# A one-core FFN down projection: one more seven-product step in the last column pair, later pair-end loads, two additions deferred, a GpSimd scratch tile of its own

## The chip, the cores and the metric

The kernel runs on one NeuronCore of one Trainium2 chip. The metric is the device time of one execution in microseconds (us). The engines are named as the profile names them: PE is TensorE (matrix products), PEld its weight loads, DVE is VectorE, ACT is ScalarE, POOL is GpSimd, and SP is SyncE, which here only issues DMAs. DMAs are issued from two queues: SP's (q1 in the profile) and POOL's (q0); only POOL's can add to what lies at the destination.

## The reference, cut to what matters

The kernel computes one decoder layer in float32 over 256 tokens: a normalisation, one input projection, eight retention heads and four mLSTM heads, an output projection, and then the part that the change touches, a gated feed-forward network (FFN) and the final normalisation:

```python
u = rmsnorm(h, norm_ffn)
up = causal_dwconv(u @ w_up, ffn_conv_w, ffn_conv_b)      # 2048 -> 2 x 5632
gate, val = jnp.split(up, [FFN_DIM], axis=-1)
h = h + (jax.nn.silu(gate) * val) @ w_down                # 5632 -> 2048
return rmsnorm(h, norm_final)[:, N_META:]
```

## The kernel before, in words

**Splitting.** Every float32 weight tile is split in two: ACT casts it to a reduced format (`whi`), DVE subtracts that from the original (`wlo`, the rest). The activations are split in the same way ahead of time. A product of weights and activations is then three matmuls: high by high, high by low, low by high. A weight tile so costs one ACT cast (L141, or L768 in the down projection's fast steps) and one DVE subtraction (L143, L770). `whi` and `wlo` have five buffers each.

**The FFN** runs in two halves of its 5632 columns. In each half first the up projection (matmuls L150, L151, L153, tiles of 512 KB loaded by L127), then the down projection, which adds to the residual stream `hn` (256 tokens in two row tiles, tt = 0 and 1; 2048 columns in four blocks of 512).

**The down projection** takes two column blocks at a time: pair `b` = 0, then pair `b` = 2. Each pair goes through eleven steps `q` over the half's rows, 256 at a time. There are two kinds of step:

- A *plain* step (0, 9 and 10) loads a raw tile for each of the two blocks (`load_plain`, into `wraw` tiles of side 0 or 1), splits both (two L143) and runs `product` for both row tiles: 24 matmuls of 512 columns (L821, L822, L824).
- A *fast* step (`seven`, steps 1 to 8) does the two-by-two block product with seven products instead of eight (after Winograd): 21 matmuls (L846, L847, L849). It needs sums of weight blocks. Part of them (`kept`) are made long before by DMAs that add in DRAM (class `Early`, four DMAs for a unit, spread over the loads of the up projection by `AHEAD` and its neighbours, with a one-element add on POOL, L210, as pace). One sum more is made by DVE in the step (L832, `ta`); another (`tb`) is loaded from `kept` by `load_sum` (L930, POOL's queue). The step's raw tile sits in `left[0]` or `left[1]`, in the tile named `hT`, and comes in three DMAs (`load_seven`, L909 by way of `load`, SP's queue). Its splits are three L770 of 1024 columns and one of 512.

Below, (b, q) is a step of a pair: hT(2,1) is the raw tile of pair 2's step 1.

**The end of a pair.** After the last fast step `share` combines the seven products' sums in `x` tiles and adds them to `hn` by four accumulating DMAs on POOL's queue (L865). After the last plain step ACT copies the pair's other accumulators out (L1003), and DVE adds them to `hn` (four L1004, which wait for those DMAs).

**The final pair** (half 1, b = 2) is different: the steps in `BOTH` are done plain, and without an early unit, so that some of its last work can be done row tile by row tile. Its order was 0, 1, 6, 2, 7, 3, 4, 5, 8, 9, 10, with 1 to 5 fast. The last four plain steps load and split one block first (one L143, twelve matmuls) and the other block later. Beside the fast steps POOL multiplies finished blocks of `hn` by the final norm's gain `gfin` (`times_gain`, L715), each released by a one-element add (L855). After the last product DVE adds the last pieces (L888), ACT and DVE make the norm's factor (L711, L720, L721, L727 to L731), and L738, L740 (DVE) and L743 (ACT) scale the rows for the output.

**What sets the order.** The program is written in the order of the code, but a list scheduler places each instruction on its engine by its own model of time; what then stands on an engine's queue is fixed, and each engine works through it in order. A DMA queue is in order too: an SP load that waits for its buffer holds all loads behind it. `tc.issue_after` ties an instruction behind another.

`raw_home` tiles have two buffers on each side; in the up projection the side of a load follows from its number: `loads % 4 // 2`.

Of the kernel before, what the change touches and what calls it, by code (L numbers as in the profile page):

```python
# [34 lines left out]
WARM = 8  # L35


AHEAD, AHEAD_STEP, REST, RESUME = 40, 22, 222, 238

# [47 lines left out]
def trunk(ctx: ExitStack, tc: tile.TileContext, io, out: bass.AP):  # L87
# [26 lines left out]


    last_load = None
    loads = paced = 0

    def raw_home(shape, side):
        return wpool.tile(shape, F32, name=f"wraw{side}", bufs=2)  # L120
# [638 lines left out]
    for half in range(2):  # L759
# [66 lines left out]
        def seven(b, q, cs, ps, first, last, after, norm):  # L826


            f = FAST.index(q)
            raw, ta, tb = homes.pop((b, q))  # L830

            nc.vector.tensor_tensor(out=ta, in0=raw[:, 0:1, :].to_broadcast([P, 2, 512]), in1=raw[:, 1:3, :], op=ALU.subtract)  # L832
            copied = None
            for w, to in (
                (raw[:, 2:4, :], ((S4, cs[0, 1], False, False), (A12, cs[0, 0], False, False))),
                (raw[:, 0:2, :], ((S2, ps[2], first, last), (A11, ps[0], first, last))),
                (ta, ((S3, ps[1], first, last), (S1, ps[3], first, last))),
                (tb, ((A22, cs[1, 0], False, False),)),
            ):
                hi = wpool.tile([P, 2, 512], F32R, name="whi", bufs=5)  # L840
                lo = wpool.tile([P, 2, 512], F32R, name="wlo", bufs=5)
                n = len(to)
                with tc.issue_after(after.ins) if first and after else nullcontext():
                    copied, _ = split(hi[:, :n, :], lo[:, :n, :], w)
                for i, (m, o, begin, _) in enumerate(to):
                    nc.tensor.matmul(o, sh[:, f, m, :], hi[:, i, :], start=begin, stop=False)  # L846
                    nc.tensor.matmul(o, sl[:, f, m, :], hi[:, i, :], start=False, stop=False)  # L847
                for i, (m, o, _, end) in enumerate(to):
                    nc.tensor.matmul(o, sh[:, f, m, :], lo[:, i, :], start=False, stop=end)  # L849
            if norm:  # L850

                with tc.issue_after(copied.ins):
                    for g in norm:
                        squares(*g)
                reached = nc.gpsimd.tensor_tensor(out=junk[:, 0:1], in0=tb[:, 0, 0:1], in1=tb[:, 0, 0:1], op=ALU.add)  # L855
                with tc.issue_after(reached.ins):
                    for tt, _, c0, c1 in norm:
                        times_gain(tt, c0, c1)

        def block(tt, b):  # L860
            return hn[:, tt, b * 512 : (b + 1) * 512]
# [40 lines left out]

        homes, raws = {}, {}
        begun = shared = None

        def load(to, src):
            nonlocal begun
# [18 lines left out]
        def load_sum(b, q):  # L926

            tb = sums_home[1][:, FAST.index(q) % 2, :][:, None, :]
# [8 lines left out]
        gains = []  # L937
        emptied = None
        for b in (0, 2):
            cs = {}  # L940
# [17 lines left out]
            for q in steps:  # L958
                if q in fast:
                    due = []  # L960
                    if final and q != fast[0]:
                        due, gains = gains[:1], gains[1:]
                    seven(b, q, cs, ps, q == fast[0], q == fast[-1], emptied, due)
                    if q == fast[-1]:
                        with tc.high_priority() if final else nullcontext():
                            shared = share(ps, b, final)
                else:
                    for j in range(1 if q in alone else 2):
                        w = split_step(raws.pop((b + j, q)))
                        for tt in range(2):  # L970
                            product(cs[tt, j], tt, q, w, q == plain[0], q == plain[-1 - (lag if final and (tt, j) == (1, 1) else 0)])

                if final:
                    if q == 0:
                        load_plain(b, 6, 0)
                    elif q == 6:
                        load_plain(b, 7, 0, 1)
                    elif q in (3, 4, 5):
                        load_plain(b, q + 5, 0 if q < 5 else 1, 1)
                    if q in (1, 2, 3):  # L980
                        load_seven(b, q + 2)
                        load_sum(b, q + 2)
                else:
                    if q == 6:
                        load_plain(b, 9, 0)
                    if q in range(1, 7):
                        load_seven(b, q + 2)
                        load_sum(b, q + 2)
                    if q == 8:
                        load_plain(b, 10, 1)  # L990
                    if b == 0:
                        if q == 7:
                            load_seven(2, 1)
                        elif q == 9:
                            load_plain(2, 0, 0)
                            load_seven(2, 2)
            for j in range(2):
                for n, tt in enumerate(range(2)):
                    c = (b + j) * 512
                    if not final:  # L1000

                        x = x_tile((4, 3, 1, 0)[2 * j + n])
                        emptied = nc.scalar.copy(x, cs[tt, j])  # L1003
                        nc.vector.tensor_tensor(out=block(tt, b + j), in0=block(tt, b + j), in1=x, op=ALU.add)  # L1004
# [117 lines left out]
```

## Time and profile before

| what | value |
|---|---|
| three runs | 1213.59, 1210.86, 1211.42 us (median 1211.42) |
| the profiled execution | 1212.01 us, its span 1210.2 us |
| granted clock of PE, mean | 0.998 |
| PE busy | 1198.8 us (99%) |
| DVE busy | 951.6 us (79%) |
| ACT busy | 713.4 us (59%) |
| POOL busy | 258.7 us (21%) |
| DMA queue q1 (SP) | 239.06 MB, 58.0% of the 16 engines' span |
| DMA queue q0 (POOL) | 37.11 MB, 17.5% |

The profiled execution is one run of its own; its span is the time from the first to the last recorded instruction, and 1.8 us of its device time lie outside. Times inside it are counted from the span's start. A row of the timeline has the start, the duration, the engine, the line and operation, output<-inputs, and how many of them follow one another; in brackets stands the engine's idle time before it and what released it. In rows of DMA issues the time is that of issuing; "to landing" is the time from the issue until the data was there. In this profile the first half's pair change lies at 763 to 779 us, the second half's at 1131 to 1149, and the last matmul at 1202.

### The profile page before, as it was taken

The page shows a single profiled execution, that of the slowest core. Times are in us where ns is not written, and L with a number is a line of the kernel's source. Part 1 is how long each engine was busy: PE and PEld are TensorE (multiplying, and loading weights), DVE is VectorE, ACT ScalarE, POOL GpSimd, SP SyncE. Part 2 cuts the span into 40 slices and gives each one's busy share as a digit, 9 for nine tenths or more (in the row PEclk, how much of TensorE's full clock was granted, in tenths as well). Part 3 has the DMA queues.
Part 4 walks back from the last instruction along what each step waited for, and adds up shares of the span by engine and source line. Part 5 has one row for each costly group of instructions (what it writes and reads, how often), then busy time and mean ns, then how long its engine had stood idle before and what let it go on. Part 6 is the DMA issues. An engine that isn't in the chain of part 4 may idle for free.

```text
span 1210.2 us, 23069 instructions
## 1 busy us (share of the span) xinstructions
PE 1198.8 (99%) x8947; PEld 1150.3 (95%) x8947; DVE 951.6 (79%) x1390; ACT 713.4 (59%) x973; POOL 258.7 (21%) x349
## 2 busy tenths in 40 slices
PE   9999999999999999999999999999999999999997
PEld 9999999999999999999999998878999999998786
DVE  8877778766775867788889779897877777778896
ACT  8657746656556556555555557665655555556673
POOL 0100022223231322233132100101133223300132
PEclk9999999999999999999999999999999999999999
DMA  7765677878786977788887757777888778847955
GB/s 278 263 224 159 203 235 210 254 217 238 209 244 208 260 223 222 238 256 227 237 229 224 233 181 261 229 249 228 271 228 252 240 222 237 221 161 265 291 195 183
DMA packets 102366, 278.50 MB, mean 230 GB/s; under 512 B 16432, under 2 KB 20656, under 8 KB 102128
## 3 DMA queue, kind: packets, MB, share of 16 engines
q1 hardware_dynamic: 84016, 239.06, 58.0%
q0 software_dynamic: 17664, 37.11, 17.5%
q8 instruction: 70, 1.15, 0.4%
q10 hardware_dynamic: 576, 0.85, 0.2%
q14 instruction: 40, 0.33, 0.1%
HBM read 268.59 MB, written 42.47 MB: 257 GB/s over the span
## 4 chain that ended last, share of the span: by engine, by line
PE 95%; DMA 2%; DVE 1%; ACT 0%; issue 0%; SPq 0%; DVEq 0%; ACTq 0%
PE mmps L150 25%; PE mmps L153 25%; PE mmps L151 25%; PE atps L821 2%; PE mmps L849 2%; PE atps L822 2%; PE atps L824 2%; PE mmps L846 2%; PE mmps L847 2%; PE atps L846 1%; PE atps L847 1%; PE atps L849 1%; DMA wraw<-in_wu 1%; DVE wlo L770 1%; DMA hT<-kept 1%; PE atps L444 1%
## 5 line engine op out<-in xcount | busy, mean ns | idle before, releaser
L141 ACT CAST whi<-wraw 128x1024 fp32r<-128x1024 f32 x346 | 361.8, 1049 | 334.0 <-PE mmps L151 221.6
L143 DVE TENSOR_TENSOR wlo<-wraw,whi 128x1024 fp32r<-128x1024 f32 x346 | 430.2, 1246 | 79.0 <-ACT whi L141 74.8
L150 PE MATMUL mmps<-uh,whi 128*128 128x258 f32 x1408 | 345.3, 283 | 0.6 <-ACT whi L141 0.6
L151 PE MATMUL mmps<-ul,whi 128*128 128x258 f32 x1408 | 345.0, 281 | 0.0
L151 PEld LDWEIGHTS mmps<-ul,whi 128*128 128x128 f32 x1408 | 266.6, 189 | 0.1
L150 PEld LDWEIGHTS mmps<-uh,whi 128*128 128x128 f32 x1408 | 265.3, 188 | 0.9 <-ACT whi L141 0.8
L150 PE MATMUL mmps<-xh,whi 128*128 128x272 f32 (+2 forms) x864 | 219.7, 287 | 0.0
L151 PE MATMUL mmps<-xl,whi 128*128 128x272 f32 (+2 forms) x864 | 218.2, 285 | 0.0
L153 PE MATMUL mmps<-uh,wlo 128*128 128x258 f32 x1408 | 197.9, 283 | 0.0
L153 PEld LDWEIGHTS mmps<-uh,wlo 128*128 128x128 f32 x1408 | 181.7, 189 | 0.0
L151 PEld LDWEIGHTS mmps<-xl,whi 128*128 128x128 f32 x864 | 162.6, 188 | 0.0
L150 PEld LDWEIGHTS mmps<-xh,whi 128*128 128x128 f32 x864 | 162.5, 188 | 0.1
L210 POOL TENSOR_TENSOR pace<-whi 128x1 f32<-128x1 f32 x87 | 52.2, 600 | 429.9 <-ACT whi L141 411.8
L153 PE MATMUL mmps<-xh,wlo 128*128 128x272 f32 (+2 forms) x864 | 126.8, 285 | 0.0
L153 PEld LDWEIGHTS mmps<-xh,wlo 128*128 128x128 f32 x864 | 114.5, 188 | 0.0
L697 DVE TENSOR_TENSOR cu<-mmps,rstd 128x258 f32<-128x258 f32 x88 | 37.6, 427 | 72.9 <-PE mmps L153 72.2
L770 DVE TENSOR_TENSOR wlo<-hT,whi 128x1024 fp32r<-128x1024 f32 x58 | 69.3, 1218 | 3.5 <-ACT whi L768 3.5
L768 ACT CAST whi<-hT 128x1024 fp32r<-128x1024 f32 x58 | 59.3, 1049 | 15.7 <-DMA hT<-kept 5.3
L768 ACT CAST whi<-wraw 128x1024 fp32r<-128x1024 f32 (+1 forms) x58 | 46.6, 835 | 35.5 <-DVE wraw L832 17.7
L151 PE MATMUL mmps<-mixl,whi 128*128 128x258 f32 x256 | 63.1, 283 | 0.0
L150 PE MATMUL mmps<-mixh,whi 128*128 128x258 f32 x256 | 62.5, 283 | 0.0
L770 DVE TENSOR_TENSOR wlo<-wraw,whi 128x1024 fp32r<-128x1024 f32 (+1 forms) x58 | 53.2, 952 | 1.5 <-ACT whi L768 0.5
(272 smaller groups left out, 1768.3 us busy)
## 6 DMA issues: line engine op xcount, KB each, us to landing
wraw<-in_wu SPq DMA_DIRECT2D x176, 512.0 KB, 4.5
wraw<-in_wi SPq DMA_DIRECT2D x108, 512.0 KB, 4.5
wraw<-in_wo SPq DMA_DIRECT2D x32, 512.0 KB, 5.4
wraw<-in_wd SPq DMA_DIRECT2D x30, 512.0 KB, 5.6
kept<-in_wd SPq DMA_DIRECT2D x29, 512.0 KB, 6.8
kept<-in_wd POOLq DMA_DIRECT2D x58, 256.0 KB, 6.7
hT<-in_wd SPq DMA_DIRECT2D x29, 512.0 KB, 4.9
kept<-kept POOLq DMA_DIRECT2D x29, 256.0 KB, 5.4
```

The costliest lines, as they stand in the source:

```text
L141: nc.scalar.copy(hi, raw)
L143: nc.vector.tensor_tensor(out=lo, in0=raw, in1=hi.bitcast(F32), op=ALU.subtract)
L150: nc.tensor.matmul(ps, hi[:, k, :], xh(kk), start=kk == first, stop=False)
L151: nc.tensor.matmul(ps, hi[:, k, :], xl(kk), start=False, stop=False)
L153: nc.tensor.matmul(ps, lo[:, k, :], xh(kk), start=False, stop=kk == last)
L210: with tc.issue_after(nc.gpsimd.tensor_tensor(out=pace, in0=x, in1=x, op=ALU.add).ins):
L697: evacuated = nc.vector.tensor_tensor(out=u, in0=ps[:, :NQ], in1=rstd2, op=ALU.mult)
L768: copied = nc.scalar.copy(hi, x)
L770: return copied, nc.vector.tensor_tensor(out=lo, in0=x, in1=hi.bitcast(F32), op=ALU.subtract)
L846: nc.tensor.matmul(o, sh[:, f, m, :], hi[:, i, :], start=begin, stop=False)
L847: nc.tensor.matmul(o, sl[:, f, m, :], hi[:, i, :], start=False, stop=False)
L849: nc.tensor.matmul(o, sh[:, f, m, :], lo[:, i, :], start=False, stop=end)
```

## The change

- `BOTH` is (7, 8) instead of (6, 7, 8): the final pair does steps 1 to 6 fast, in the order 0, 1, 2, 7, 3, 4, 5, 6, 8, 9, 10. One more `Early` unit (30 instead of 29) is made for it, and `AHEAD` goes from 40 to 36 loads. `kept21`, which keeps pieces that the plain steps of `BOTH` need, is a third smaller.
- `loads`, the counter that picks the raw side, starts at 3 instead of 0.
- hT(2,1) was loaded after step 7 of pair 0; now it is loaded after step 9, on SP's queue, behind the plain tiles of steps 10 and (2,0). hT(2,2), which stood there, goes to POOL's queue behind the four accumulating DMAs.
- In the final pair, from step 3 on, `tb` is loaded on SP's queue instead of POOL's.
- Of the four L1004 adds at the end of a pair 0, the two of block j = 1 are put into a list (`later`) and issued behind the last split of pair 2's first fast step.
- `gfin` (1 MB) is no longer loaded at the start of half 1's down projection but in four pieces beside steps 3 to 6 of its first pair.
- The one-element add ahead of `times_gain` writes `pace`, not `junk`, which ACT writes too.

Lines of the FFN's helpers move by one (L143 is L144, L770 is L771, L832 is L833), later ones by more (L930 is L943, L1004 is L1023, L715 and L728 to L740 are one higher, L888 is L890).

```diff
-AHEAD, AHEAD_STEP, REST, RESUME = 40, 22, 222, 238
+AHEAD, AHEAD_STEP, REST, RESUME = 36, 22, 222, 238
...
-    loads = paced = 0
+    loads, paced = 3, 0
...
-    BOTH = FAST[-3:]
+    BOTH = FAST[-2:]
...
-                reached = nc.gpsimd.tensor_tensor(out=junk[:, 0:1], in0=tb[:, 0, 0:1], in1=tb[:, 0, 0:1], op=ALU.add)
+                reached = nc.gpsimd.tensor_tensor(out=pace, in0=tb[:, 0, 0:1], in1=tb[:, 0, 0:1], op=ALU.add)
...
-            nc.gpsimd.dma_start(gfin, io["gfin"])
...
-            load(raw[:, 2:4, :], io["wd7"][b // 2, half * NQD + q][:, 2:4, :])
-            load(raw[:, 1, :], io["wd7"][b // 2, half * NQD + q][:, 1, :])
-            load(raw[:, 0, :], early[b, half * NQD + q].kept[:, 0, :])
+            w = io["wd7"][b // 2, half * NQD + q]
+            parts = ((raw[:, 2:4, :], w[:, 2:4, :]), (raw[:, 1, :], w[:, 1, :]), (raw[:, 0, :], early[b, half * NQD + q].kept[:, 0, :]))
+            for to, src in parts:
+                if (b, q) == (2, 2):
+
+                    with tc.issue_after(shared.ins):
+                        nc.gpsimd.dma_start(to, src)
+                else:
+                    load(to, src)
...
-            with tc.issue_after(shared.ins) if shared else nullcontext():
-                nc.gpsimd.dma_start(tb[:, 0, :], early[b, half * NQD + q].kept[:, 1, :])
+            kept = early[b, half * NQD + q].kept[:, 1, :]
+            if half == 1 and b == 2 and q > 2:
+
+                load(tb[:, 0, :], kept)
+            else:
+                with tc.issue_after(shared.ins) if shared else nullcontext():
+                    summed = nc.gpsimd.dma_start(tb[:, 0, :], kept)
...
-            steps = [0, 1, 6, 2, 7, 3, 4, 5, 8, 9, 10] if final else range(NQD)
+            steps = [0, 1, 2, 7, 3, 4, 5, 6, 8, 9, 10] if final else range(NQD)
...
-                    seven(b, q, cs, ps, q == fast[0], q == fast[-1], emptied, due)
+                    done = seven(b, q, cs, ps, q == fast[0], q == fast[-1], emptied, due)
+                    if q == fast[0]:
+
+                        with tc.issue_after(done.ins):
+                            while later:
+                                later.pop(0)()
...
+                    if (half, b) == (1, 0) and q in range(3, 7):
+                        cols = slice((q - 3) * 512, (q - 2) * 512)
+                        with tc.issue_after(summed.ins):
+                            nc.gpsimd.dma_start(gfin[:, cols], io["gfin"][:, cols])
                     if b == 0:
-                        if q == 7:
+                        if q == 9:
+                            load_plain(2, 0, 0)
                             load_seven(2, 1)
-                        elif q == 9:
-                            load_plain(2, 0, 0)
                             load_seven(2, 2)
...
-                        nc.vector.tensor_tensor(out=block(tt, b + j), in0=block(tt, b + j), in1=x, op=ALU.add)
+                        later.append(lambda to=block(tt, b + j), x=x: nc.vector.tensor_tensor(out=to, in0=to, in1=x, op=ALU.add))
+                        if j == 0 or b == 2:
+                            later.pop(0)()
```

Three places show how instructions move on DVE. The first is the start of half 0's pair 0, where the up projection ends. The first sum (`wraw<-hT`), the plain step's two splits (L143, the last two) and the first fast split stood before like this:

```order
L143 TENSOR_TENSOR wlo<-wraw_9078,whi 128x1024
L697 TENSOR_TENSOR cu<-mmps,rstd_78 128x258
L143 TENSOR_TENSOR wlo<-wraw_9132,whi 128x1024
L701 SCALAR_TENSOR_TENSOR vt<-cu,par,vt 128x256 x2
L782 TENSOR_TENSOR gt<-gt,vt 128x256
L143 TENSOR_TENSOR wlo<-wraw_9134,whi 128x1024
L770 TENSOR_TENSOR ml<-gt,mh 128x256
L832 TENSOR_TENSOR wraw_9142<-hT 128x1024
```

and now:

```order
L144 TENSOR_TENSOR wlo<-wraw_9083,whi 128x1024
L833 TENSOR_TENSOR wraw_9147<-hT 128x1024
L698 TENSOR_TENSOR cu<-mmps,rstd_78 128x258
L144 TENSOR_TENSOR wlo<-wraw_9137,whi 128x1024
L702 SCALAR_TENSOR_TENSOR vt<-cu,par,vt 128x256 x2
L144 TENSOR_TENSOR wlo<-wraw_9139,whi 128x1024
```

The sum moved ahead of the plain step's two splits.

The second is the change from pair 0 to pair 2 in half 0 (half 1 has the same, but for the second sum, which now stands ahead of the 512-column split). `hn<-hn,x` are the adds at the pair's end. Before:

```order
L143 TENSOR_TENSOR wlo<-wraw_9524,whi 128x1024
L143 TENSOR_TENSOR wlo<-wraw_9558,whi 128x1024
L832 TENSOR_TENSOR wraw_9613<-hT 128x1024
L143 TENSOR_TENSOR wlo<-wraw_9560,whi 128x1024
L1004 TENSOR_TENSOR hn<-hn,x_5926 128x512 x4
L770 TENSOR_TENSOR wlo<-hT,whi 128x1024 x2
L770 TENSOR_TENSOR wlo<-wraw_9613,whi 128x1024
L770 TENSOR_TENSOR wlo<-wraw_9614,whi 128x512
L832 TENSOR_TENSOR wraw_9613<-hT 128x1024
```

Now:

```order
L144 TENSOR_TENSOR wlo<-wraw_9526,whi 128x1024
L144 TENSOR_TENSOR wlo<-wraw_9560,whi 128x1024
L144 TENSOR_TENSOR wlo<-wraw_9562,whi 128x1024
L833 TENSOR_TENSOR wraw_9616<-hT 128x1024
L1023 TENSOR_TENSOR hn<-hn,x_5931 128x512 x2
L771 TENSOR_TENSOR wlo<-hT,whi 128x1024 x2
L771 TENSOR_TENSOR wlo<-wraw_9616,whi 128x1024
L771 TENSOR_TENSOR wlo<-wraw_9617,whi 128x512
L1023 TENSOR_TENSOR hn<-hn,x_5931 128x512 x2
L833 TENSOR_TENSOR wraw_9616<-hT 128x1024
```

Two of the adds moved behind step 1's splits, and step 1's sum behind the last plain split.

The third is the end of the program on DVE. The 256-column `hn<-atps,hn` rows are the last adds of row tile 0 and of row tile 1, each followed by links of its norm factor; L740 and L738 scale. Before:

```order
L740 TENSOR_SCALAR hn<-hn,frt 128x256
L740 TENSOR_SCALAR hn<-hn,frt 128x768
L738 SCALAR_TENSOR_TENSOR hn<-hn,frt,gfin 128x512
L720 TENSOR_REDUCE rest<-ss_5925 128x1
L721 TENSOR_SCALAR rest<-rest 128x1
L888 TENSOR_TENSOR hn<-atps,hn 128x256
L728 TENSOR_SCALAR frt<-ss_5925,rest 128x1
```

Now:

```order
L890 TENSOR_TENSOR hn<-atps,hn 128x256
L741 TENSOR_SCALAR hn<-hn,frt 128x256
L741 TENSOR_SCALAR hn<-hn,frt 128x768
L739 SCALAR_TENSOR_TENSOR hn<-hn,frt,gfin 128x512
L729 TENSOR_SCALAR frt<-ss_5930,rest 128x1
```

Row tile 0's scaling moved behind the last add.

More of the change, by code (lines that the diff above doesn't have):

```diff
@@ L843, in seven @@
                 with tc.issue_after(after.ins) if first and after else nullcontext():
-                    copied, _ = split(hi[:, :n, :], lo[:, :n, :], w)
+                    copied, parted = split(hi[:, :n, :], lo[:, :n, :], w)
                 for i, (m, o, begin, _) in enumerate(to):
@@ L858, in seven @@
                         times_gain(tt, c0, c1)
+            return parted
         def block(tt, b):
@@ L903, in trunk @@
         homes, raws = {}, {}
-        begun = shared = None
+        begun = shared = summed = None
         def load(to, src):
@@ L920, in load_seven @@
             turn = 1 - turn
[L921 to L923 removed]
+            w = io["wd7"][b // 2, half * NQD + q]
[6 more added lines that the diff above has]
+                    load(to, src)
             homes[b, q] = raw
         def load_sum(b, q):
+            nonlocal summed
             tb = sums_home[1][:, FAST.index(q) % 2, :][:, None, :]
[L929 to L930 removed]
+            kept = early[b, half * NQD + q].kept[:, 1, :]
[4 more added lines that the diff above has]
+                    summed = nc.gpsimd.dma_start(tb[:, 0, :], kept)
             homes[b, q] = homes[b, q], sums_home[0], tb
@@ L936, in trunk @@
         lag = 4
-        gains = []
+        gains, later = [], []
         emptied = None
@@ L974, in trunk @@
                     if q == 0:
-                        load_plain(b, 6, 0)
-                    elif q == 6:
                         load_plain(b, 7, 0, 1)
-                    elif q in (3, 4, 5):
-                        load_plain(b, q + 5, 0 if q < 5 else 1, 1)
-                    if q in (1, 2, 3):
+                    elif q in (4, 5, 6):
+                        load_plain(b, q + 4, 0 if q < 6 else 1, 1)
+                    if q in range(1, 5):
                         load_seven(b, q + 2)
```

## The prediction, made before the changed kernel ran

> **What bounds the kernel now.** I read the page first (who is busy, which queues carry the bytes), then busy time by stretch, then the timeline of each place that the change touches.
>
> ```profile
> PE 1198.8 (99%) x8947; PEld 1150.3 (95%) x8947; DVE 951.6 (79%) x1390; ACT 713.4 (59%) x973; POOL 258.7 (21%) x349
> ...
> PEclk9999999999999999999999999999999999999999
> ```
> ```profile
> core 0: us, PE busy (x) PEld busy (x) DVE busy (x) ACT busy (x) POOL busy (x), PEclk, DMA share, GB/s
> 725.00:763.00 38.00, 38.00 (x165) 30.56 (x164) 36.58 (x36) 26.87 (x31) 2.69 (x5) 1.00 0.72 235
> 763.00:779.00 16.00, 16.00 (x70) 12.87 (x69) 12.24 (x16) 8.88 (x12) 4.64 (x6) 1.00 1.01 290
> 779.00:824.00 45.00, 44.03 (x185) 34.15 (x184) 42.99 (x42) 28.55 (x33) 4.14 (x7) 1.00 0.63 214
> 1149.00:1184.00 35.00, 35.00 (x152) 28.16 (x151) 34.51 (x29) 23.74 (x32) 12.24 (x11) 1.00 0.56 194
> ```
>
> PE works through 99% of the span at full clock: only fewer matmuls, shorter PE waits or a shorter tail can save time. But DVE, 79% over the span, is full just where the change works: 36.58 of 38, 42.99 of 45 and 34.51 of 35 us. Only at the pair's end (763 to 779) does it rest, 12.24 of 16, while the DMA engines are full (share 1.01).
>
> PE's waits at these places, and its pitch:
>
> ```profile
> 782.29 0.62 PE L849 MATMUL atps<-wlo,sh 128*128 128x512 f32 x2
> ...
> 814.45 0.63 PE L849 MATMUL mmps<-wlo,sh 128*128 128x512 f32 x2
> 815.87 0.51 PE L846 MATMUL atps<-whi,sh 128*128 128x512 f32 x1 [0.79 <-ACT whi L768]
> ...
> 818.56 0.51 PE L846 MATMUL mmps<-whi,sh 128*128 128x512 f32 x1 [0.16 <-ACT whi L768]
> ...
> 835.34 0.65 PE L153 MATMUL mmps<-uh,wlo 128*128 128x258 f32 x4
> 836.54 0.39 PE L150 MATMUL mmps<-uh,whi 128*128 128x258 f32 x1 [0.56 <-ACT whi L141]
> 836.77 0.29 PE L151 MATMUL mmps<-ul,whi 128*128 128x258 f32 x1
> 836.89 0.28 PE L150 MATMUL mmps<-uh,whi 128*128 128x258 f32 x1
> ...
> 1128.73 0.86 PE L849 MATMUL atps<-wlo,sh 128*128 128x512 f32 x3
> 1129.78 0.50 PE L846 MATMUL mmps<-whi,sh 128*128 128x512 f32 x1 [0.18 <-ACT whi L768]
> ...
> 1182.35 0.40 PE L822 MATMUL atps<-whi,sl 128*128 128x512 f32 x1
> ...
> 1183.05 0.39 PE L849 MATMUL atps<-wlo,sh 128*128 128x512 f32 x1
> ```
>
> From 1182.35 to 1183.05 lie three pitches: 0.233 us for a matmul of 512 columns; the 258-column one has 0.12 (836.77 to 836.89). A fast step is 21 x 0.233 = 4.9 us of PE, a plain one of two blocks 24 x 0.233 = 5.6. Against these pitches PE lost 0.95 us ahead of 815.87 (the idle shown there is less, since a matmul's end lies behind its pitch), at least 0.16 ahead of 818.56, 0.7 ahead of 836.54 and 0.35 ahead of 1129.78.
>
> DVE's price of a fast step, and what lengthens it:
>
> ```profile
> 782.89 1.22 DVE L832 TENSOR_TENSOR wraw<-hT 128x1024 f32<-128x1024 f32 x1
> ...
> 803.77 1.22 DVE L832 TENSOR_TENSOR wraw<-hT 128x1024 f32<-128x1024 f32 x1
> ...
> 1148.65 2.36 DVE L770 TENSOR_TENSOR wlo<-hT,whi 128x1024 fp32r<-128x1024 f32 x2
> ...
> 1165.88 1.81 DVE L770 TENSOR_TENSOR wlo<-wraw,whi 128x1024 fp32r<-128x1024 f32 x2
> 1167.62 2.31 DVE L832 TENSOR_TENSOR wraw<-hT 128x1024 f32<-128x1024 f32 x1
> ...
> 1178.37 1.81 DVE L770 TENSOR_TENSOR wlo<-wraw,whi 128x1024 fp32r<-128x1024 f32 x2
> 1180.10 3.44 DVE L143 TENSOR_TENSOR wlo<-wraw,whi 128x1024 fp32r<-128x1024 f32 x2
> ```
> ```profile
> 1166.22 0.92 POOL L855 TENSOR_TENSOR junk<-wraw 128x1 f32<-128x1 f32 x1 [2.59 <-ACT junk L711]
> 1167.11 1.74 POOL L715 TENSOR_TENSOR hn<-hn,gfin 128x512 f32<-128x512 f32 x1
> ```
>
> Between the two L832 rows at 782.89 and 803.77 lie four steps: 20.88 / 4 = 5.22 us of DVE for each, more than PE's 4.9. So in a run of fast steps DVE loses 0.32 us of lead a step; a plain step (two L143, 2.3 us) gives 3.3 back. L832 took 2.31 us instead of 1.22 where the gain product L715 ran on POOL: +1.1 us each.
>
> **The change, part by part.**
>
> *One plain step becomes fast:* three matmuls fewer, 3 x 0.233 = **-0.7 us**.
>
> *The raw tiles' turn starts at 3.* At the half's end a second up tile can be loaded behind plain step 9, where only one could. The wait ahead of 836.54 is for the cast of such a tile: **-0.7** (0 if the next tile is late instead).
>
> *gfin in four pieces, and a shorter kept21 copy.* Half 1's first pair no longer meets a 1 MB load at its start; the wait at 1129.78, the last of DVE's lost lead, goes: **-0.35** (0 to -0.7). The pieces come to the same megabyte beside steps 3 to 6, in which PE has no such wait.
>
> *Pair end of half 0.* The sums' loads:
>
> ```profile
> 764.59 0.99 SPq L909 DMA_DIRECT2D hT<-in_wd  x2
> 765.63 0.72 SPq L909 DMA_DIRECT2D hT<-kept  x1
> ...
> DMA to landing us min/median/max: 9.8/11.3/12.8
> ```
> ```profile
> 774.13 1.29 DVE L1004 TENSOR_TENSOR hn<-hn,x 128x512 f32<-128x512 f32 x2
> 776.24 0.69 DVE L1004 TENSOR_TENSOR hn<-hn,x 128x512 f32<-128x512 f32 x1 [0.82 <-DMA hn<-x]
> 778.27 0.69 DVE L1004 TENSOR_TENSOR hn<-hn,x 128x512 f32<-128x512 f32 x1 [1.34 <-DMA hn<-x]
> 778.88 2.35 DVE L770 TENSOR_TENSOR wlo<-hT,whi 128x1024 fp32r<-128x1024 f32 x2
> ```
>
> These three loads are hT(2,2), behind four plain tiles on SP; the last landed at 765.63 + 12.8 = 778.4. hT(2,1) had come long before, so its sum stood ahead of the adds. The change puts hT(2,1) in exactly this place of SP's queue, and its sum L833 before the first split. What DVE did in its wait now waits itself. DVE enters the run of pair 0 one sum earlier (1.14 us), and the loads follow its splits, so I take 777.3 for the landing: then L833 1.14, two adds 1.29, and the splits start at 779.7 instead of 778.88; the two deferred adds behind step 1 make DVE 0.85 + 1.29 = 2.1 us late for the steps after it. The lead was 782.29 - (778.88 + 1.22) = 2.2 at step 1, and seven steps use 7 x 0.32 = 2.2: nothing is left over. The waits ahead of 815.87 and 818.56, 0.95 + 0.16 = 1.1 us (the 779 to 824 row has 0.97 of PE idle), lie in the same chain and are already paid: 2.1 - 1.1 = **+1.0**. Bounds: -1.1, if the landing is so early that the waits vanish; +3.3, if it stays at 778.4 and the step-8 load slips along.
>
> The split between queues gains little by the rows: 763 to 779 has every DMA engine at work. The Trainium skill (DMA: Bandwidth & Descriptors, Issuing engines are not separate DMA queues) says that another issuing engine saves only issue time, since all run on the same 16 DMA engines. By that the landing would stay at 778.4 and this term be 1.14 more, +2.1.
>
> *Final pair.* hT(2,2) landed here at:
>
> ```profile
> 1135.71 0.44 SPq L909 DMA_DIRECT2D hT<-kept  x1
> ...
> DMA to landing us min/median/max: 10.5/11.9/13.0
> ```
> ```profile
> 1151.35 0.63 PE L849 MATMUL atps<-wlo,sh 128*128 128x512 f32 x2
> ```
>
> 1135.71 + 13.0 = 1148.7. DVE is freer in half 1's first pair; I take 1.6 us of that for the loads, so 1147.1, and the first split of step 1 ends at 1147.1 + 1.14 + 1.29 + 1.22 = 1150.75: lead 0.6, where it was 1.5. From there to the last split of the last fast step DVE took 1149.87 to 1180.18 = 30.3 us, PE 1151.35 to 1183.05 = 31.7. Now PE has 31.0. DVE adds 5.22 for the fast step less 2.28 for the plain one, 1.29 of deferred adds, and half of a 1.1 (the fourth gain product fell behind this stretch, at 1180.10, and may now fall into it): 35.1. 0.6 + 31.0 - 35.1 = -3.5: PE waits **+3.5**. Bounds: +0.5 (landing 2 us earlier still and one product hidden), +5.5 (landing at 1148.7, four products). It ends in a wait of PE for wlo in steps 3 to 6.
>
> A row stands against a larger price: the one-column add L855 at 1166.22 did not lengthen the splits beside it (1.81 for two, as at 1178.37). The Trainium skill (SBUF: State Buffer, Who interferes with whom) says a DVE instruction with two SBUF inputs contends with any GpSimd instruction that reads SBUF, whole instruction against whole instruction. By that the four pace-writing adds would cost too, some 4 x 0.9 us by the row's length, and the term be +7; the row shows none of it, so I leave it.
>
> *tb on SP, pace instead of junk.* SP waits for a free half of tb ahead of the next hT, which waits longer anyway for its own buffer; POOL's waits on ACT's junk were off the path: 0. If that cover failed, a step would see its load late by one add, 0.7 us, inside the +5.5. The 30th Early unit's four loads and three pace adds lie under up steps in which PE never waits: 0, or one late tile, 0.7.
>
> *Tail.*
>
> ```profile
> 1199.99 0.89 DVE L740 TENSOR_SCALAR hn<-hn,frt 128x256 f32<-128x256 f32 x2
> 1200.79 1.23 DVE L738 SCALAR_TENSOR_TENSOR hn<-hn,frt,gfin 128x512 f32<-128x512 f32 x1
> ...
> 1202.25 0.42 DVE L888 TENSOR_TENSOR hn<-atps,hn 128x256 f32<-128x256 f32 x1
> 1203.25 0.21 DVE L728 TENSOR_SCALAR frt<-ss,rest 128x1 f32<-128x1 f32 x1 [0.58 <-ACT junk L711]
> ```
>
> The first row tile's scaling (L740, L738) ran ahead of the last add; in the new order it stands behind it and ahead of L729, the next link of the end's chain. After the add at 1202.6 it takes 0.85 + 1.2 = 2.05, so L729 starts at 1204.7 instead of 1203.25: **+1.45** (0 if the last add comes late anyway, 2.1 if the bunched output stores also slow).
>
> **Sum:** -0.7 - 0.7 - 0.35 + 1.0 + 3.5 + 1.45 = +4.2. The profiled execution took 1212.01 us (span 1210.2 and 1.8 around it), so 1216.2 for it; it stands 0.6 above the median 1211.42, so **1215.6 us**.
>
> **Rivals.**
>
> *The loads do spread (faster).* Without hT(2,1) in the middle of pair 0, the plain tiles and then hT(2,1) land some 3 us sooner than hT(2,2) did, before DVE is through its L143s. Then the half-0 waits go (-1.1), the final pair costs +0.5, and the tail nothing: -0.7 - 0.7 - 0.7 - 1.1 + 0.5 = -2.7, **1208.7**. For it: hT(2,1)'s megabyte left the stretch before 761. Against: SP issued the plain tiles only when DVE freed their buffers, and the accumulates come no earlier than PE. It decides where hT(2,1) lands before 774.2, when DVE finishes its last L143.
>
> *They cancel.* Landing at about 776 and 1146: half 0 level, final pair +1.5, tail +1.45, the three savings -1.75: +1.2, less up to 1 us if the tail's scaling finds a gap: about **1212**.
>
> *The queues collide.* hT(2,2) and both tb queue on POOL behind four accumulates, so step 1's last split and step 2's sum wait as well: upper bounds of both pairs, -1.75 + 3.3 + 5.5 + 1.45 = +8.5, **1219.9**. For it: hT(2,2) took 12.8 us to land in this crowd. Against: the lead of DVE in step 1 hides a load that is late by less than two splits.
>
> **Numbers.** Forecast 0.40, cancel 0.25, loads spread 0.20, collision 0.15. The range leaves out half of the last and the end of the faster case: 1208.8 to 1219.0. A measurement of this kernel can tell about 0.2%, 2.4 us, from no change: faster 0.2, same 0.25, slower 0.55.
>
> **What would show it.** Right: DVE idle ahead of L833 after the last L143 until hT lands (about 777 and 1147); PE waits for wlo or whi in steps 2 to 8 of pair 2 and, 3 to 4 us in sum, in the final pair; L741 between the last L890 and L729; no wait near 836. Wrong: a landing before 774, DVE never idle there, or a final pair in which PE shows no wait.

## The result and the profile after

The changed kernel took 1221.34 us (median of six runs, 1219.87 to 1225.92) against 1211.26 for the kernel before on the same chips: ratio 1.0087, interval 1.0069 to 1.0106. It is slower by 10 us. That way was forecast, but not so far: 1215.6, with a range that ended at 1219.0.

The page of the changed kernel and its busy time by stretch (same columns as before; the whole runs later now, so the stretches are moved by what PE had lost up to there):

```profile
PE 1200.4 (98%) x8944; PEld 1149.8 (94%) x8944; DVE 953.6 (78%) x1392; ACT 713.4 (59%) x974; POOL 266.5 (22%) x361
```
```profile
764.00:780.00 16.00, 16.00 (x70) 12.85 (x70) 8.82 (x10) 7.98 (x10) 6.27 (x9) 1.00 1.04 293
780.00:828.00 48.00, 45.29 (x189) 34.41 (x188) 46.87 (x47) 29.82 (x34) 4.14 (x7) 1.00 0.65 224
1151.00:1192.00 41.00, 36.64 (x151) 27.30 (x150) 40.88 (x38) 24.70 (x34) 11.67 (x9) 1.00 0.59 194
```

Three matmuls fewer and PE ends later. DVE (third figure behind the stretch's length) rests more than before at the pair's end, 8.82 busy of 16 us where it was 12.24, and then runs without a gap: 46.87 of 48, and 40.88 of 41 in the final pair, in which PE was idle for 4.4 us. Work moved off the one stretch where DVE had time into those where it had none.

Where the 9.3 us between the two spans (1219.5 and 1210.2) arose is read from the start of the same matmul, by its count from the first, in both traces. The stretches end, in the kernel before, at 776.7 (in the plain step that opens half 0's pair 2), 831.3 (the end of half 0), 1083.1 (in half 1's up projection), 1147.6 (in the plain step that opens the final pair), 1202.2 (the last matmul's end) and 1210.2 (the end):

| kernel | to 776.7 | pair 2, half 0 | up to half 1 | pair 0, half 1 | final pair | end | sum |
|---|---|---|---|---|---|---|---|
| changed | +1.4 | +2.35 | -0.8 | -0.7 | +5.5 | +1.6 | +9.3 |
| e1, pair-end loads as before | +0.3 | -1.1 | -0.9 | +0.3 | +4.7 | +1.7 | +5.0 |
| e2, adds as before | +0.6 | +1.4 | -0.8 | -0.5 | +5.9 | +1.0 | +7.6 |
| e3, step 6 plain | +0.6 | +3.1 | -0.9 | +0.4 | +3.6 | +0.4 | +7.2 |
| e4, both of e1 and e3 | +0.6 | -1.0 | -0.8 | +0.1 | 0.0 | +0.4 | -0.6 |
| e5, no gain products | +1.1 | +3.2 | -0.8 | +1.8 | +3.2 | +1.6 | +10.1 |
| e6, e1 without gain products | +0.9 | -0.5 | -0.8 | +0.5 | -0.65 | +1.8 | +1.3 |
| e7, hT(2,1) ahead of (2,0) | +0.3 | +0.5 | -0.8 | +3.3 | +2.8 | +1.7 | +7.8 |
| e8, hT(2,2) on SP | -0.1 | +1.8 | -0.9 | +0.7 | +6.8 | +1.7 | +10.0 |
| e9, turn only | +0.2 | +0.6 | -0.8 | +0.3 | 0.0 | 0.0 | +0.3 |
| e10, turn and deferred adds | +0.2 | -0.4 | -0.8 | +0.8 | 0.0 | 0.0 | -0.2 |
| e11, gfin in pieces only | 0.0 | -0.4 | -0.7 | +1.0 | 0.0 | 0.0 | -0.1 |
| e12, before without products | +0.7 | -1.4 | -0.8 | -0.2 | 0.0 | 0.0 | -1.8 |

Each row is one profiled execution, against one of the kernel before. The last four rows say how far that goes: these kernels are nearly the one before, and they are off it by up to 0.7, 1.4, 0.8 and 1.0 us in the first four columns and by nothing in the last two. The third column is about -0.8 in every row, so what it shows is a wait of the kernel before's one execution.

The pair's end, in the timeline of the changed kernel, first DVE's, then SP's last load of hT(2,1) with the landing times of its three loads, then the same of half 1:

```profile
774.28 1.23 DVE L144 TENSOR_TENSOR wlo<-wraw,whi 128x1024 fp32r<-128x1024 f32 x1 [1.39 <-ACT whi L142]
780.10 1.23 DVE L833 TENSOR_TENSOR wraw<-hT 128x1024 f32<-128x1024 f32 x1 [4.60 <-DMA hT<-kept]
781.24 1.29 DVE L1023 TENSOR_TENSOR hn<-hn,x 128x512 f32<-128x512 f32 x2
782.45 2.35 DVE L771 TENSOR_TENSOR wlo<-hT,whi 128x1024 fp32r<-128x1024 f32 x2
784.72 1.82 DVE L771 TENSOR_TENSOR wlo<-wraw,whi 128x1024 fp32r<-128x1024 f32 x2
786.46 1.28 DVE L1023 TENSOR_TENSOR hn<-hn,x 128x512 f32<-128x512 f32 x2
```
```profile
767.14 0.84 SPq L910 DMA_DIRECT2D hT<-kept  x1
...
DMA to landing us min/median/max: 9.8/11.3/12.8
```
```profile
1136.77 0.85 SPq L910 DMA_DIRECT2D hT<-kept  x1
...
DMA to landing us min/median/max: 10.0/11.5/13.0
```
```profile
1149.85 1.23 DVE L833 TENSOR_TENSOR wraw<-hT 128x1024 f32<-128x1024 f32 x1 [4.03 <-DMA hT<-kept]
```

DVE is through its plain splits at 775.5 and stands still for 4.60 us until hT(2,1) lands at 767.14 + 12.8 = 780.0; in half 1 it is 4.03. Then come the sum, two adds, the splits and two more adds, as forecast. The 12.8 us from issue to landing are those that hT(2,2) took in this place before. From there to 819 us in half 0, and to 1189 us in half 1, DVE waited for no load.

The final pair: what PE waited for, and the last fast step of DVE, ACT and PE:

```profile
PE mmps L847 <- ACT whi L769: 3.6, 3, 1.5
PE atps L850 <- DVE wlo L771: 0.7, 1, 0.7
```
```profile
1184.91 1.21 DVE L833 TENSOR_TENSOR wraw<-hT 128x1024 f32<-128x1024 f32 x1
...
1187.31 1.83 DVE L771 TENSOR_TENSOR wlo<-wraw,whi 128x1024 fp32r<-128x1024 f32 x2
```
```profile
1186.24 1.57 ACT L769 CAST whi<-wraw 128x1024 fp32r<-128x1024 f32 x2 [3.30 <-DVE wraw L833]
```
```profile
1190.71 0.39 PE L850 MATMUL atps<-wlo,sh 128*128 128x512 f32 x1
```

PE's row names ACT's cast, but ACT itself waited 3.30 us for DVE's sum L833: the bound is DVE. The prediction's term for this pair had named `wlo`, DVE's splits; for the most part (3.6 of 4.3 us) it was the cast of DVE's sum. And the order within a step matters: PE needs the cast of the sum (L833, then ACT) ahead of the last splits, so that when the last split was done at 1187.31 + 1.83 = 1189.14, PE used it only at 1190.71. A lead of 1.57 us was left that PE could not use.

The products that stop DVE:

```profile
1160.94 2.92 DVE L771 TENSOR_TENSOR wlo<-wraw,whi 128x1024 fp32r<-128x1024 f32 x2
...
1176.42 2.32 DVE L833 TENSOR_TENSOR wraw<-hT 128x1024 f32<-128x1024 f32 x1
```
```profile
1161.03 2.28 POOL L716 TENSOR_TENSOR hn<-hn,gfin 128x512 f32<-128x512 f32 x1
...
1175.91 1.75 POOL L716 TENSOR_TENSOR hn<-hn,gfin 128x512 f32<-128x512 f32 x1
```

Two splits took 2.92 us where the pair without a product beside it took 1.83 (1187.31), the sum 2.32 instead of 1.21: 1.1 us each again, and all four products fell into fast steps.

The end:

```profile
1210.04 0.16 DVE L732 SCALAR_TENSOR_TENSOR frt<-frt,fr 128x1 f32<-128x1 f32 x1
1210.12 0.42 DVE L890 TENSOR_TENSOR hn<-atps,hn 128x256 f32<-128x256 f32 x1
...
1211.25 0.74 DVE L739 SCALAR_TENSOR_TENSOR hn<-hn,frt,gfin 128x512 f32<-128x512 f32 x1
1211.91 0.20 DVE L729 TENSOR_SCALAR frt<-ss,rest 128x1 f32<-128x1 f32 x1
...
1212.66 1.14 DVE L741 TENSOR_SCALAR hn<-hn,frt 128x256 f32<-128x256 f32 x3
```
```profile
1209.26 0.73 POOL L716 TENSOR_TENSOR hn<-hn,gfin 128x256 f32<-128x256 f32 x1 [3.06 <-ACT junk L712]
```

and two rows of the kernel before:

```profile
1204.26 1.14 DVE L740 TENSOR_SCALAR hn<-hn,frt 128x256 f32<-128x256 f32 x3
```
```profile
1200.44 1.03 POOL L715 TENSOR_TENSOR hn<-hn,gfin 128x256 f32<-128x256 f32 x1 [2.74 <-ACT junk L711]
```

L741 and L739 of row tile 0 do stand between L890 and L729. From the last add's start to the last scaling (L741 x3) it is 2.54 us, where it was 1204.26 - 1202.25 = 2.01: +0.5, not +1.45. L729 started 1.79 us after the add's start, where L728 had 1.00: only 0.8 later, since the gain scaling L739 took 0.74 us here. The 1.2 that the prediction used is L738's time beside a 256-column gain product on POOL (1200.44); now that product was over by 1210.0. Another 0.3 came back behind L729, because ACT's part of the chain had meanwhile been done. The rest of the 1.6 is 0.2 by which the last add started later after the last matmul, and 0.9 of output: the last store landed 4.3 us after its issue, with the other row tile's stores beside it, where it was 3.4 before.

### The profile page after: what moved, and what is told of

The parts are those of the page before. It is cut to its first block, busy times and chain, and to the rows that moved or that the text cites. A ratio compares the mean times of both kernels' runs of the same rounds, so it can differ in the third digit from the quotient of the medians.

```text
span 1219.5 us, 23083 instructions
## 1 busy us (share of the span) xinstructions
PE 1200.4 (98%) x8944; PEld 1149.8 (94%) x8944; DVE 953.6 (78%) x1392; ACT 713.4 (59%) x974; POOL 266.5 (22%) x361
## 4 chain that ended last, share of the span: by engine, by line
PE 93%; DMA 3%; DVE 2%; issue 1%; ACT 1%; SPq 0%; DVEq 0%; ACTq 0%
PE mmps L151 25%; PE mmps L154 25%; PE mmps L152 25%; PE mmps L847 2%; PE mmps L850 2%; PE mmps L848 2%; DMA hT<-kept 2%; PE atps L822 2%; PE atps L823 2%; PE atps L825 2%; PE atps L848 1%; PE atps L847 1%; PE atps L850 1%; DVE wlo L771 1%; PE atps L445 1%
## 5 line engine op out<-in xcount | busy, mean ns | idle before, releaser
L144 DVE TENSOR_TENSOR wlo<-wraw,whi 128x1024 fp32r<-128x1024 f32 x344 | 427.3, 1244 | 82.7 <-ACT whi L142 78.5
L211 POOL TENSOR_TENSOR pace<-whi 128x1 f32<-128x1 f32 x90 | 57.4, 638 | 420.7 <-ACT whi L142 411.7
L771 DVE TENSOR_TENSOR wlo<-hT,whi 128x1024 fp32r<-128x1024 f32 x60 | 71.8, 1217 | 2.6 <-ACT whi L769 2.6
L771 DVE TENSOR_TENSOR wlo<-wraw,whi 128x1024 fp32r<-128x1024 f32 (+1 forms) x60 | 58.4, 1007 | 1.6 <-PE mmps L850 0.7
```

What stands on the lines that cost most here:

```text
L144: nc.vector.tensor_tensor(out=lo, in0=raw, in1=hi.bitcast(F32), op=ALU.subtract)
L211: with tc.issue_after(nc.gpsimd.tensor_tensor(out=pace, in0=x, in1=x, op=ALU.add).ins):
L771: return copied, nc.vector.tensor_tensor(out=lo, in0=x, in1=hi.bitcast(F32), op=ALU.subtract)
```

## The experiments

The theory (A) was that DVE is the bound in pair 2 of both halves, because hT(2,1) lands late and because of the sixth fast step with its products. The rivals gave the whole loss to one of these, to the deferred adds, or to the raw tiles' turn. Times are medians, with the ratio to the kernel before on the same chip.

**e1, the pair-end loads as before.**

```diff
-                        if q == 9:
-                            load_plain(2, 0, 0)
+                        if q == 7:
                             load_seven(2, 1)
+                        elif q == 9:
+                            load_plain(2, 0, 0)
                             load_seven(2, 2)          # and (2,2) through load(), on SP
```

> The changed kernel, but hT(2,1) loaded after step 7 again and hT(2,2) on SP's queue, as before. Theory A (the late landing of hT(2,1) is what makes DVE late, in both halves): DVE's 4.6 and 4.0 us of idle time ahead of the first sum of pair 2 go, PE's waits fall from 4.4 to about 2 us in half 0's pair 2 and from 6.0 to about 2 in the final pair: about 1215. Rival B (six fast steps are too much DVE work wherever the loads stand): the final pair keeps 5 us or more of waits, only half 0 gains its 1.6: about 1219.5.

Measured: 1216.52, ratio 1.0050 (1.0037 to 1.0064). Half 0's loss is gone (+2.35 to -1.1), so there theory A holds. The final pair kept most of its own (+5.5 to +4.7), as rival B said. Its row shows why:

```profile
1171.33 3.44 DVE L771 TENSOR_TENSOR wlo<-hT,whi 128x1024 fp32r<-128x1024 f32 x2
1174.69 2.90 DVE L771 TENSOR_TENSOR wlo<-wraw,whi 128x1024 fp32r<-128x1024 f32 x2
```
```profile
1154.12 12.10 POOL L856 TENSOR_TENSOR pace<-wraw 128x1 f32<-128x1 f32 x1 [4.54 <-DMA wraw<-kept]
...
1171.41 4.50 POOL L716 TENSOR_TENSOR hn<-hn,gfin 128x512 f32<-128x512 f32 x2
```

DVE began this pair with its lead, and lost it where the products came one behind the other. They came so because the one-column add that releases the first of them had a span of 12.10 us in this execution, so that all four products fell between 1166 and 1176 us. DVE had no gap during that add; whether the one held the other up is not shown.

**e2, all four adds at the pair's end** (`later.pop(0)()` always, without its condition).

> The changed kernel with all four adds at the pair's end again. Theory A: DVE's sum of work up to step 2 is the same, only its order differs, so PE's waits in both pairs stay within 1 us of the changed kernel's; the end's scaling stands ahead of the last add in this build, which gives back 1.5: about 1220. Rival C (the deferral itself is what delays steps 2 and later): waits fall by 1.3 in each half: about 1217.

Measured: 1222.78, ratio 1.0099 (1.0085 to 1.0113). The deferral is not to blame; rival C falls. (The profiled execution took 1219.62, 3 us less than the median, so the row in the table does not hold all of the loss.) Two things of the expectation failed. The time is not lower. And the end was longer by 1.0 although the scaling stood ahead of the last add: row tile 0 was ready so late that the scaling held the last add up instead. So the end's price is not that of the order alone.

**e3, step 6 plain again** (`BOTH = FAST[-3:]`, the old order, `AHEAD` 40).

> The changed kernel with step 6 of the final pair plain again (BOTH, order and AHEAD as before). Theory A: step 6 plain gives DVE 2.9 us and PE 0.7, so the final pair's 6.0 us of waits fall to about 2, not to nothing, because hT(2,1) still lands late; half 0's stay at 4.4; the end's 1.5 goes: about 1216.5. Rival B: the final pair's waits go to nothing: about 1214.5.

Measured: 1217.85, ratio 1.0062 (1.0049 to 1.0075). The final pair's loss fell from 5.5 to 3.6 with the late loads alone in place: more than the 2 expected, and not the nothing of rival B. The end's price went (+1.6 to +0.4). `AHEAD` and the 30th early unit went back with the step; they act in the up projections, and the first and third columns do not tell the rows with them from those without.

**e4, both as before**; kept are the turn, the deferred adds, gfin in pieces, `tb` on SP's queue and the pace tile.

> Pair-end loads and step 6 as before; kept are the turn of the raw tiles, the two deferred adds, gfin in pieces, the pace tile. Theory A: the waits ahead of 836 and 1129 us stay gone (1.4 us) and the deferred adds free DVE at the pair's end, so half 0's 2.8 us of waits shrink too: 1208.5 to 1210. Rival D (the raw turn or the new gfin loads cost something elsewhere, as the 1.4 us that PE lost in the first 10 us of the changed kernel may say): about 1211.

Measured: 1210.63, ratio 1.0002 (0.9993 to 1.0011). All of the 10 us lies in the pair-end loads and the sixth fast step. What is kept is worth nothing that can be measured, gain or loss: the expected 1208.5 to 1210 did not come. The parts overlap: e3 against e4 (the loads alone) costs 7.2 us, e1 against e4 (the step alone) 5.9, together 10.7.

**e5, no gain products beside the fast steps** (the four `times_gain` calls and their `reached` adds in `seven` left out, so these blocks leave without the final norm's gain).

> The changed kernel without the four gain products on POOL beside the final pair's fast steps, and without the adds that release them (so these blocks leave without the final norm's gain). Theory A (the products stop DVE, 1.1 us each, and all four now fall where DVE has no lead): the final pair's waits fall from 6.0 by 4.4 to about 1.6: about 1217. Rival E (the products only fill time in which DVE would wait for loads or casts anyway): waits stay above 4: about 1220.

Measured: 1217.48, ratio 1.0057 (1.0045 to 1.0070), 3.9 us below the changed kernel, as theory A has it. The profiled execution itself took 1222.1, so the sum in the table is higher than the median's difference; hT(2,1) landed there 13.6 and 14.1 us after its issue. The final pair's waits lay before 1162 us, at its start; after that PE did not wait, where the changed kernel lost some 4 us.

**e6, e1 and e5 together** (the gain is left out here too).

> Pair-end loads as before and no gain products on POOL beside the fast steps (the same blocks leave without the gain); the sixth fast step stays. Theory A: 5.3 us of waits in the final pair minus 4.4: about 1 left: about 1212. Rival B (the sixth fast step is too much for DVE by itself): 3 us or more left: 1214 or more.

Measured: 1212.51, ratio 1.0012 (1.0004 to 1.0021). Busy time of the final pair in e1 (first row) and e6 (second):

```profile
1149.00:1186.00 37.00, 34.80 (x146) 26.60 (x145) 36.80 (x34) 22.63 (x33) 23.20 (x9) 1.00 0.55 183
```
```profile
1150.00:1185.00 35.00, 35.00 (x151) 28.16 (x151) 34.10 (x35) 24.06 (x33) 1.81 (x2) 1.00 0.65 212
```

Without products PE is never idle, though DVE is at 34.10 of 35: theory A, and rival B falls as stated. Six fast steps fit, but with nothing to spare, and what the sixth wins (0.7 us of matmuls, the -0.65 in the table) the end takes back (+1.8). So even without the products it is no gain.

**e7, hT(2,1) ahead of the plain tiles of (2,0)** (`load_seven(2, 1)` one line up).

> The changed kernel, but behind step 9 hT(2,1) is loaded ahead of the plain tiles of (2,0), which have over 4 us of lead. Theory A (the landing follows the megabytes ahead of it on SP's queue): hT(2,1) lands 3 to 4 us earlier, DVE's idle time ahead of the first sum goes, half 0's waits fall from 4.4 to under 2, the final pair's from 6.0 to about 5: about 1218. Rival F (the landing is set by the accumulates and PE's pace, not by the queue's order): nothing changes, 1221.

Measured: 1220.69, ratio 1.0078 (1.0066 to 1.0090). Rival F's time, but not its reason. The loads did land early, at most 6.8 us after their issue and not 12.8:

```profile
DMA to landing us min/median/max: 6.4/6.6/6.8
```
```profile
770.44 1.23 DVE L833 TENSOR_TENSOR wraw<-hT 128x1024 f32<-128x1024 f32 x1 [0.68 <-DMA hT<-kept]
774.12 1.22 DVE L144 TENSOR_TENSOR wlo<-wraw,whi 128x1024 fp32r<-128x1024 f32 x1 [2.46 <-ACT whi L142]
```
```profile
1143.89 1.04 ACT L142 CAST whi<-wraw 128x1024 fp32r<-128x1024 f32 x1 [7.42 <-DMA wraw<-in_wd]
1144.85 1.07 ACT L1022 COPY x<-atps 128x512 f32<-128x512 f32 x2
```
```profile
PE atps L822 <- ACT x L1022: 1.9, 1, 1.9
```

The sum could start at 770.4 instead of 780.1. Now the plain tiles are late; in half 1 ACT waited 7.42 us for one, with the copies L1022 queued behind it, and PE waited for those copies: +3.3 in the column of half 1's pair 0, while pair 2 of half 0 fell from +2.35 to +0.5 and the final pair from 5.5 to 2.8. The wait had, for the most part, changed its place.

**e8, hT(2,2) on SP's queue behind hT(2,1).**

> The changed kernel, but hT(2,2) goes to SP's queue behind hT(2,1), instead of POOL's. Theory A with the skill's rule (the issuing queue changes nothing while all 16 engines are full): hT(2,1) lands within 0.5 us of the changed kernel's time against the accumulates, waits as in the changed kernel: 1221. Rival G (the POOL queue behind the accumulates delays hT(2,2) and both tb, or relieves SP): hT(2,2) lands 2 us or more earlier or later and half 0's waits move by over 1: 1219 or 1223.

Measured: 1222.74, ratio 1.0095 (1.0082 to 1.0108). The three loads of hT(2,1) took:

```profile
DMA to landing us min/median/max: 9.5/11.1/12.5
```

against 9.8/11.3/12.8 with hT(2,2) on POOL. hT(2,2) itself was there at 783.1 us on SP's queue and at 783.7 on POOL's, and DVE waited for it on neither. The queue made no difference, as theory A has it: what counts, by e7, is what was issued ahead of it. The Trainium skill (DMA: Bandwidth & Descriptors, Issuing engines are not separate DMA queues) says the same of the issuing engine: DMAs from all of them run on the same 16 DMA engines, and another one saves only the time of issuing.

**e9 to e12, one part each on the kernel before.** e9: `loads, paced = 3, 0`. e10: that and the two adds deferred. e11: gfin in four pieces. e12: nothing but the four gain products and their adds left out (these blocks leave without the gain).

> The kernel before with the raw tiles' turn starting at 3, nothing else. Theory A: the wait ahead of 836 us goes (0.8), PE's first 14 us stay within 0.5 of the kernel before (the 1.1 that the changed kernel lost there was chance): about 1210.2. Rival D (the turn costs 1.1 at the start): about 1211.3, with the loss seen in the first 14 us.

> The kernel before with the turn starting at 3 and the two adds deferred; gfin in one load, tb and the pair-end loads as before. Theory A: the wait near 836 goes (0.8) and half 0's pair 2 loses 1 of its 2 us of waits, since DVE starts step 1's splits before the last accumulate has landed: about 1209. Rival H (what is gained there comes back in the end, as in the run with both back): 1210.6.

> The kernel before with gfin in four pieces beside steps 3 to 6 of half 1's first pair, nothing else. Theory A: the 0.7 us of waits near 1129 go: about 1210.3. Rival I (the pieces delay the loads of steps 6 to 9 by as much as the one load delayed those of steps 1 and 2, as the 0.75 to 1.4 us of waits between 1090 and 1148 in most of the other runs say): 1211, with waits of 0.5 us or more there.

> The kernel before without the four gain products on POOL beside the final pair's fast steps, and without the adds that release them (these blocks leave without the gain). Theory A (a product costs DVE 1.1 us but PE only where DVE has no lead; five fast steps among two plain ones leave it one): no change, within 0.5 us of 1211. Rival J (the products cost PE time in any order): 1209 or less.

Measured: e9 1210.46, ratio 0.9996 (0.9987 to 1.0005); e10 1211.77, 1.0004 (0.9995 to 1.0012); e11 1211.02, 0.9999 (0.9990 to 1.0008); e12 1210.91, 0.9996 (0.9987 to 1.0005). None can be told from the kernel before. e9: no loss at the start, against rival D; the 1.4 us that the changed kernel's profiled execution lost in its first 10 us came from the first load, which landed 1.4 us later; e6, with the same instructions there, lost 0.9 in the same way and e8 nothing. The wait near 836 us is gone as expected, but not because of the turn, as e11 and e12 show: there the turn is as before and the wait is gone nevertheless. ACT's cast ahead of which PE had waited, in the kernel before and in e12:

```profile
835.44 1.05 ACT L141 CAST whi<-wraw 128x1024 fp32r<-128x1024 f32 x1 [3.16 <-DMA wraw<-in_wu]
```
```profile
833.46 1.05 ACT L142 CAST whi<-wraw 128x1024 fp32r<-128x1024 f32 x1 [1.93 <-DMA wraw<-in_wu]
```

The tile had come 2 us sooner (0.75 of which because e12 was that far ahead by then), with no edit that bears on it: the wait was that one execution's. e11 did not lose its waits near 1129 but had +1.0 there, as rival I said. e12 is theory A's control: with five fast steps among the plain ones the products cost PE nothing (final pair 0.0), with six they cost about 4 (3.9 by e5, 4.0 by e6 against e1).

No version beat the kernel before by more than can be measured.

## Why the prediction was too small

The mechanism was the one forecast: DVE is late in pair 2 of both halves, because hT(2,1) lands late and, in the final pair, because of the sixth fast step with its products. What failed is the size of two terms, the final pair's and half 0's pair 2, and in the second the way it was worked out. In the profiled execution the sum was 5.1 us short (+4.2 against +9.3): 2.7 of that lies in the final pair, 1.35 in half 0's pair 2 and 1.4 at the kernel's start, less 0.3 over the rest. In the order of the sum:

- **One plain step becomes fast, -0.7:** right (e6: -0.65).
- **The turn, -0.7:** the cause was wrong. The wait at 836 us was read as the turn's; e11 and e12 lose it without the turn. The changed kernel shows -0.8 there, as every other trace does within 0.2. A gain of 0.7 us is too small for the medians (e9's interval reaches from -1.6 to +0.6 us).
- **gfin in pieces, -0.35:** -0.7 in this execution, +1.0 in e11 alone: chance. The step that failed in both is the same: a wait under 1 us in one execution was taken for one that every execution has.
- **Half 0's pair 2, +1.0; measured +2.35.** Two steps failed here. The first is the landing: "the loads follow its splits, so I take 777.3". It was 780.0 in a program that ran 1.4 us later, so 778.6, no sooner than before. The sum had moved ahead at the start of pair 0, but SP's issue had not: 762.68 - 1.37 = 761.3, as before. So DVE was 2.1 + 1.3 = 3.4 us late. The second is the subtraction: the waits ahead of 815.87 and 818.56 were not "already paid". In both kernels they end with the load of step 8's raw tile, hT(2,8), which SP issues into the buffer of step 6's raw tile when DVE has split that. Before and after:

```profile
807.71 0.39 SPq L909 DMA_DIRECT2D hT<-kept  x1
...
816.12 1.23 DVE L832 TENSOR_TENSOR wraw<-hT 128x1024 f32<-128x1024 f32 x1 [1.82 <-DMA hT<-kept]
```
```profile
812.42 0.44 SPq L910 DMA_DIRECT2D hT<-kept  x1
...
819.85 1.22 DVE L833 TENSOR_TENSOR wraw<-hT 128x1024 f32<-128x1024 f32 x1 [0.81 <-DMA hT<-kept]
```

  PE waits for the cast of this sum in both. DVE's delay comes on top of such a wait in full: the load was issued 812.42 - 1.37 - 807.71 = 3.3 us later, which is the term's upper bound, "+3.3, if it stays at 778.4 and the step-8 load slips along". It landed 7.2 us after its issue instead of 8.3, and so the sum began only 2.36 us later. That 1.0 + 1.3 makes 2.3 too is a coincidence. In all traces the column "pair 2, half 0" follows the landing of this one load within 0.3 us; it took 6.4 to 8.7 us from one execution to the next, for no reason that the runs show.
- **Final pair, +3.5; measured +6.2** (+5.5 and the 0.7 that the step saved). DVE's work from the first sum to the last split was sized right: the prices used, 6 x 5.22 + 2 x 1.29 + 1.14 + 4 x 1.1, make 39.4 us, and 1149.85 to 1189.14 is 39.3. Three things were missing: PE cannot use the last 1.57 us of a lead, since it waits for the sum's cast earlier in the step; all four products fell into the stretch, not three and a half (+0.55); and the landing was 0.5 later than taken (1136.77 + 13.0 less the 2.2 lost up to there is 1147.6). 3.5 + 1.57 + 0.55 + 0.5 = 6.1. A sign of the first was there before: the wait at 818.56, too, was for the cast of a sum and not for a split.
- **End, +1.45; measured +1.6,** but of 0.5 in DVE's chain, 0.2 ahead of it and 0.9 in the stores, where the first alone was forecast: the size is right by luck. e2 shows that the order is not the cause by itself.
- **Not in the sum:** 1.4 us at the start, which was chance.

Of the rivals, "the loads do spread" and "they cancel" are refuted by the changed kernel's own trace: hT(2,1) landed at 778.6 and 1147.6, counted as above, and neither before 774.2 nor at 776 and 1146. "The queues collide" came near in size, 1219.9, with the wrong mechanism: hT(2,2) and both `tb` stood behind the accumulates, but DVE waited for none of them, and hT(2,2) on SP's queue (e8) changed nothing. What the forecast said the profile would show, it does: DVE idle ahead of L833, PE's waits in pair 2, L741 between the last L890 and L729, no wait near 836. The range ended at 1219.0 because it left out half of the collision, the only case in which both pairs took their upper bounds. But landing, products and the unusable lead all lie on DVE's one chain and add up without any collision.

## What to carry to other kernels

When an engine that is 79% busy over the span is full in the stretch that you change, count its work there from the event that starts it to the use that ends it, and find the lead that the consumer can't use. A wait that the profile already shows behind that engine is no credit: a further delay of the engine adds to it in full. In these runs a load took its landing time from its place in the queue (hT(2,1) that of hT(2,2)), and putting another one first moved the wait to what was now last (e7). Small waits of one execution are confirmed in a second one before a term rests on them.

## What was not expected of the hardware

The price of a POOL product to DVE was the same wherever one met it, 1.1 us for a 512-column product that itself took 1.3 to 2.3 us, and 0.5 for one of 256 columns; whether PE paid it went with DVE's lead (nothing in e12, about 4 us in e5 and e6). One-column POOL adds cost DVE nothing that can be seen, but one of them had a span of 12.10 us while DVE ran without a gap (e1), where four such adds took 0.4 to 1.8 us in the kernel before. One of the first loads (a 128x640 tile of `in_w`) landed 5.8 us after its issue in the changed kernel's profile and 4.4 to 5.4 in the others, with the same instructions ahead of it: up to 1.4 us at the kernel's start that no edit made.
